# Merge products behind the sixth head, the first norm's weights spread by TensorE, and another order of the first transfers, in a two-layer encoder kernel

## The chip, the cores and the metric

The kernel runs on one core of one Trainium2 chip. The metric is the device time in microseconds of one execution, start to end. Several executions are timed and the median is taken; lower is better. One more execution is taken with the hardware profiler, and all rows in this document that are not of a timing come from such an execution.

## The reference

A trunk of two layers on 256 tokens of width 1024, all in float32. Cut to what matters:

```python
def reference(x, positions, norm_w, w_in, ...):
    angles = positions[..., None] * inv_freq
    cos, sin = jnp.cos(angles), jnp.sin(angles)
    for l in range(DEPTH):                                # DEPTH = 2
        h = rmsnorm(x, norm_w[l])                         # x: (1, 256, 1024)
        proj = h @ w_in[l]                                # one input projection for both branches
        (q_a, k_a, v_a, ab_a, z_a, q_b, k_b, v_b, z_b, gate_a, gate_b) = split(proj)
        y_a = gated_delta_branch(q_a, k_a, v_a, ab_a, z_a, ...)   # 8 heads, both directions, triangular solves
        y_b = diff_attention_branch(q_b, k_b, v_b, z_b, cos, sin, ...)  # 8 heads, two softmaxes each
        merged = sigmoid(gate_a) * (y_a @ w_pa[l]) + sigmoid(gate_b) * (y_b @ w_pb[l])
        x = x + merged @ w_out[l]
    return rmsnorm(x, final_norm_w)
```

`rmsnorm(x, w)` is `x * rsqrt(mean(x*x) + 1e-6) * w`.

## The kernel before, in words

Tokens are two tiles of 128 partitions (m = 0, 1). A projection multiplies the normalised, transposed input hT by 512 columns of weights. For precision each operand is split into a high and a low part in float32r, and three products are summed: high by high, high by low, low by high. Weights come in four parts of 512 KB (`raw`, three buffers). ScalarE (ACT) casts a part to its high half (line 233), VectorE (DVE) subtracts to get the low half (line 235), and TensorE (PE) runs 6 products of a token tile on a part, each 512 columns wide. A projection is 48 such products.

A planner orders the instructions of each engine from a simulated timeline. Program order is the priority, and within it a block `with behind(ins)` (or `tc.issue_after(ins)`) puts an instruction behind `ins` in the queue of the same engine. On the chip each engine runs its queue in that fixed order and waits by semaphores.

**The start.** SP's DMA queue issues, in this order: the two halves of token tile 0 (line 314), the norm's weights spread over all 128 partitions (`wb_n`, 512 KB, line 166), the two halves of tile 1, three weight parts of the first projection `vb` (line 224), and, once a buffer is free, the fourth part. `normed` squares a tile on ACT (line 177), adds the two sums on DVE (line 179), takes the power -0.5 on GpSimd (POOL, lines 161 and 162), and multiplies tile, factor and weights on DVE (line 189). `split_T` transposes on PE (line 199), copies the high part on ACT (205) and subtracts for the low part on DVE (206). `proj_by_tile` (line 261) then runs tile 0 over all eight row blocks (kt) and tile 1 after it, in that order on PE (line 275). The position arithmetic for the rotary embedding (lines 124 to 148) is small DVE work traced before all this.

**The merge.** In the middle of each layer, unit triangular blocks of 32 are solved on DVE (lines 619 and 620), written to device memory and read back in another layout, as `T64` (line 654) and `U_` (line 658). A generator `merges(g)`, one for each half of the heads, then joins blocks on PE: y64p (line 672), zt64 (686) and z64 (692), y128p (709), zt128 (717), each followed by copies on ACT. `step(mg)` advances both generators by one stage. Between the stages the attention heads stand, `head(h)`: scores `sc` (788), exponentials on ACT (797), transposes `at` (808), copy `aT` (810), the product with the values `av` (814). `mark["av"]` holds the last `av` product traced so far, `mark["proj"]` the last product of a projection. After the merge come `chunks`, the gated output, its transposes `pt_ya`, and the projection `pp_pa`; the projections `za`, `gb`, `pb` and `ga` supply PE's other work meanwhile.

## Time and profile before

| what | value |
|---|---|
| median of 3 runs | 793.67 us (792.81 to 794.49) |
| the profiled execution's own time | 795.0 us |
| its span, first to last instruction | 793.3 us |
| PE busy | 757.1 us, 95% of the span |
| DVE / ACT / POOL busy | 559.7 / 478.9 / 98.0 us |
| mean granted PE clock | 0.994 |
| DMA moved | 127.44 MB, 161 GB/s |

How to read rows: a timeline row is start, duration (us), engine, line, operation, output<-inputs, shape, count, and in brackets the idle time before it with what ended it. A wait row is "engine line waited for: total us, times, longest us". A chain row is start, length (us), engine and group. A tile's row of DMA issues gives the issuing queue's ns (min/median/max) and the first and last start in us, followed by a row of the time from issue to landing. A windows row is a stretch, its length, busy us of PE, PE's weight load, DVE, ACT and POOL with counts, granted clock, DMA share and GB/s.

### The profile page before, as it was taken

The page shows a single profiled execution, that of the slowest core. Times are in us where ns is not written, and L with a number is a line of the kernel's source. Part 1 is how long each engine was busy: PE and PEld are TensorE (multiplying, and loading weights), DVE is VectorE, ACT ScalarE, POOL GpSimd, SP SyncE. Part 2 cuts the span into 40 slices and gives each one's busy share as a digit, 9 for nine tenths or more (in the row PEclk, how much of TensorE's full clock was granted, in tenths as well). Part 3 has the DMA queues.
Part 4 walks back from the last instruction along what each step waited for, and adds up shares of the span by engine and source line. Part 5 has one row for each costly group of instructions (what it writes and reads, how often), then busy time and mean ns, then how long its engine had stood idle before and what let it go on. Part 6 is the DMA issues. An engine that isn't in the chain of part 4 may idle for free.

```text
span 793.3 us, 13809 instructions
## 1 busy us (share of the span) xinstructions
PE 757.1 (95%) x5218; PEld 650.0 (82%) x5218; DVE 559.7 (71%) x1053; ACT 478.9 (60%) x1043; POOL 98.0 (12%) x133
## 2 busy tenths in 40 slices
PE   4989999999999999999989899999999999999996
PEld 3988889887778988878769799799777789897874
DVE  5487978999973553666655978889999537447564
ACT  4557776556777655553534687765667775565443
POOL 6000371100030100100010015501001100001000
PEclk9999999999999999999999999999999999999999
DMA  6565757554494534355754467556455934435561
GB/s 200 166 186 147 199 178 209 160 171 146 111 206 126 159 127 133 107 178 183 224 166 129 143 181 242 159 171 174 146 159 140 196 99 154 132 110 158 184 208 58
DMA packets 77888, 127.44 MB, mean 161 GB/s; under 512 B 19694, under 2 KB 20030, under 8 KB 77822
## 3 DMA queue, kind: packets, MB, share of 16 engines
q1 hardware_dynamic: 73886, 116.79, 49.5%
q0 software_dynamic: 3936, 9.77, 4.6%
q8 instruction: 41, 0.67, 0.4%
q14 instruction: 25, 0.20, 0.1%
HBM read 121.79 MB, written 4.75 MB: 160 GB/s over the span
## 4 chain that ended last, share of the span: by engine, by line
PE 66%; DVE 14%; DMA 8%; ACT 7%; issue 3%; POOL 1%; SPq 0%; POOLq 0%; ACTq 0%; DVEq 0%
PE pp_qk L248 3%; PE pp_qk L249 3%; PE pp_vb L275 2%; PE pp_qk L247 2%; PE pf_v L290 2%; PE pp_gb L247 2%; ACT B L577 2%; PE pf_v L294 2%; PE pf_v L292 2%; PE pp_gb L248 2%; PE pp_pb L248 2%; PE pp_gb L249 2%; PE pp_pb L247 2%; PE pp_pb L249 2%; PE pf_k L294 2%
## 5 line engine op out<-in xcount | busy, mean ns | idle before, releaser
L248 PE MATMUL pp_qk<-lo_qk,hT 128*128 128x512 f32 x128 | 51.3, 401 | 1.0 <-DVE lo_qk L235 1.0
L249 PE MATMUL pp_qk<-hi_qk,hT 128*128 128x512 f32 x128 | 50.0, 391 | 0.0
L235 DVE TENSOR_TENSOR lo_qk<-raw_qk,hi_qk 128x1024 fp32r<-128x1024 f32 x32 | 40.2, 1256 | 9.0 <-ACT hi_qk L233 8.7
L247 PE MATMUL pp_qk<-hi_qk,hT 128*128 128x512 f32 x128 | 46.1, 398 | 0.4 <-ACT hi_qk L233 0.4
L233 ACT CAST hi_qk<-raw_qk 128x1024 fp32r<-128x1024 f32 x32 | 33.5, 1047 | 20.0 <-PE pp_qk L249 12.6
L235 DVE TENSOR_TENSOR lo_pb<-raw_pb,hi_pb 128x1024 fp32r<-128x1024 f32 x16 | 19.6, 1225 | 31.3 <-ACT hi_pb L233 31.3
L235 DVE TENSOR_TENSOR lo_gb<-raw_gb,hi_gb 128x1024 fp32r<-128x1024 f32 x16 | 19.6, 1223 | 30.2 <-ACT hi_gb L233 30.2
L290 PE MATMUL pf_v<-hT,hi_v 128*128 128x256 f32 x128 | 36.5, 288 | 0.0
L290 PE MATMUL pf_q<-hT,hi_q 128*128 128x256 f32 x128 | 36.3, 287 | 0.0
L292 PE MATMUL pf_v<-hT,hi_v 128*128 128x256 f32 x128 | 36.2, 285 | 0.0
L797 ACT ACTIVATE es<-sc,mx 128x256 f32<-128x256 f32 x64 | 29.8, 472 | 10.4 <-DVE mx L795 10.3
L292 PE MATMUL pf_q<-hT,hi_q 128*128 128x256 f32 x128 | 35.8, 284 | 0.0
L290 PE MATMUL pf_k<-hT,hi_k 128*128 128x256 f32 x128 | 35.6, 283 | 0.0
L292 PE MATMUL pf_k<-hT,hi_k 128*128 128x256 f32 x128 | 35.6, 283 | 0.0
L294 PE MATMUL pf_q<-hT,lo_q 128*128 128x256 f32 x128 | 35.2, 290 | 0.0
L294 PE MATMUL pf_v<-hT,lo_v 128*128 128x256 f32 x128 | 34.5, 285 | 0.0
L294 PE MATMUL pf_k<-hT,lo_k 128*128 128x256 f32 x128 | 34.3, 286 | 0.0
L235 DVE TENSOR_TENSOR lo_pa<-raw_pa,hi_pa 128x1024 fp32r<-128x1024 f32 x16 | 19.6, 1224 | 18.7 <-ACT hi_pa L233 18.7
L235 DVE TENSOR_TENSOR lo_k<-raw_k,hi_k 128x1024 fp32r<-128x1024 f32 x16 | 19.6, 1224 | 18.0 <-ACT hi_k L233 18.0
L235 DVE TENSOR_TENSOR lo_ga<-raw_ga,hi_ga 128x1024 fp32r<-128x1024 f32 x16 | 19.4, 1224 | 16.0 <-ACT hi_ga L233 16.0
L476 DVE SCALAR_TENSOR_TENSOR cvk<-pf_k,cw,cvk 128x254 f32<-128x254 f32 (+1 forms) x64 | 29.2, 478 | 2.0 <-ACT cvk L472 1.2
L233 ACT CAST hi_pa<-raw_pa 128x1024 fp32r<-128x1024 f32 x16 | 16.9, 1054 | 22.4 <-PE pp_pa L249 18.9
(361 smaller groups left out, 2520.9 us busy)
## 6 DMA issues: line engine op xcount, KB each, us to landing
raw_qk<-in_w_in_dram SPq DMA_DIRECT2D x32, 512.0 KB, 3.7
raw_vb<-in_w_in_dram SPq DMA_DIRECT2D x16, 512.0 KB, 3.8
raw_k<-in_w_in_dram SPq DMA_DIRECT2D x16, 512.0 KB, 3.7
raw_q<-in_w_in_dram SPq DMA_DIRECT2D x16, 512.0 KB, 3.7
raw_v<-in_w_in_dram SPq DMA_DIRECT2D x16, 512.0 KB, 3.8
raw_zb<-in_w_in_dram SPq DMA_DIRECT2D x16, 512.0 KB, 3.6
raw_za<-in_w_in_dram SPq DMA_DIRECT2D x16, 512.0 KB, 3.6
raw_gb<-in_w_in_dram SPq DMA_DIRECT2D x16, 512.0 KB, 4.2
```

What stands on the lines that cost most here:

```text
L233: S.copy(hi[:, :, :n], raw[:, :, :n])
L235: V.tensor_tensor(lo[:, :, :n], raw[:, :, :n], hi[:, :, :n].bitcast(F32), ALU.subtract)
L247: T.matmul(o, act[kt // 4][:, 0, kt % 4, ts_], hi, start=kt == 0, stop=False)
L248: T.matmul(o, act[kt // 4][:, 0, kt % 4, ts_], lo, start=False, stop=False)
L249: mark["proj"] = T.matmul(o, act[kt // 4][:, 1, kt % 4, ts_], hi, start=False, stop=kt == KT - 1).ins
L275: mark["proj"] = T.matmul(o, a_, w_, start=kt == 0 and a_ is ah and w_ is hi, stop=kt == KT - 1 and a_ is al).ins
L290: T.matmul(o, hi[:, cs], act[kt // 4][:, 0, kt % 4, :], start=first, stop=False, skip_group_check=True)
L292: T.matmul(o, hi[:, cs], act[kt // 4][:, 1, kt % 4, :], start=False, stop=False, skip_group_check=True)
L294: T.matmul(o, lo[:, cs], act[kt // 4][:, 0, kt % 4, :], start=False, stop=done, skip_group_check=True)
L476: V.scalar_tensor_tensor(ca[:, o0:o1], acc[:, b, o0 + sft : o1 + sft], cw[:, j, cb : cb + 1], ca[:, o0:o1], ALU.mult, ALU.add)
L577: S.activation(dec[:, d, j4, :], dec[:, d, j4, :], AF.Exp, bias=lnc[:, d, c, h : h + 1])
L797: S.activation(es[:, n, qt, :], spv[:, qt, :], AF.Exp, bias=mx[:, n, qt : qt + 1], accum_out=s_all[:, h, n, qt : qt + 1])
```

## The change

Three edits.

1. The first layer's norm weights are read as one row of 4 KB on ACT's DMA queue (`norm_row`), and two PE products with a row of ones spread it over the partitions into two PSUM banks. DVE reads them there. All other norms keep the spread transfer.
2. The first transfers and the order of the first projection. SP issues tile 0, weight part 0, tile 1 (`tokens(1)`, called when row block 2 is reached), weight part 1. Parts 2 and 3 are issued on ACT's queue behind tile 0's squares (`held`). Parts 1 and 3 take buffers of the tag `w4a` (`spare`), so that all four have a buffer at once. The order on DVE is written out: low half of part 0 behind tile 0's last norm product; low half of part 1 behind tile 0's last transposed low half; tile 1's sum and norm products behind the low half of part 1; low halves of parts 2 and 3 behind tile 1's last norm product. The position arithmetic and the memset of `U_` are traced after the first projection, the former behind tile 1's last norm product.
3. In the merge, `head(4)` and `head(5)` both stand before the third step, and the first y64p product of half 0 is put behind `mark["av"]` (head 5's last) instead of `mark["proj"]`.

```diff
+    def norm_row(w_row, nm):
+        row = work.tile([P, DM], F32, tag="w4c", name=f"wr_{nm}", bufs=3)
+        nc.scalar.dma_start(out=row[0:1, :], in_=w_row.unsqueeze(0))
+        wb = [bank(f"wb_{nm}{i}") for i in range(2)]
+        for i in range(2):
+            T.matmul(wb[i], tri[0:1, 0, :], row[0:1, 512 * i : 512 * i + 512], start=True, stop=True)
+        return wb
...
-        V.tensor_tensor(r, ss[:, 0:1], ss[:, 1:2], ALU.add)
+        with behind(after):
+            V.tensor_tensor(r, ss[:, 0:1], ss[:, 1:2], ALU.add)
...
+        sq = norm_factor(xt_, m, h, r, ss, range(2), after and mark["norm", 0][1])
...
+            with behind(after):
+                hh = V.scalar_tensor_tensor(h[:, cs], xt_[i][:, m, :], r, wb[i],
+                                            ALU.mult, ALU.mult).ins
...
+                if kp in spare:
+                    raw = work.tile([P, 2, 512], F32, tag="w4a", name=f"raw_{nm}{kp}", bufs=2)
+                else:
+                    raw = wpool.tile([P, 2, 512], F32, tag="raw", name=f"raw_{nm}{kp}", bufs=3)
+                with behind(mark["norm", 0][0] if kp in held else None):
+                    (nc.scalar if kp in held else nc.sync).dma_start(
+                        out=raw[:, :, :n], ...)
...
+        if l == 0:
+            later[0] = None, mark["norm", 0][1]
+            def between(kt):
+                if kt == 2:
+                    tokens(1)
+                    later[1] = None, mark["split", 0, 1][1]
+                elif kt == 4:
+                    prenorm(1, xt, wb, 0, mark["parts"])
+                    later[2] = later[3] = None, mark["norm", 1][1]
...
         for _ in proj_by_tile(hT, wl, C_VB, evac_v(0), f"vb{l}0", places,
-                              later=later, turn=...):
+                              later=later, spare=() if l else (1, 3), held=() if l else (2, 3), between=between,
+                              turn=...):
...
-            first = mark["proj"] if g == 0 else None
+            first = mark["av"] if g == 0 else None
...
         step(mg)
         step(mg)
-        step(mg)
         head(4)
+        head(5)
         step(mg)
         step(mg)
         step(mg)
-        head(5)
+        step(mg)
         in_step(chunks(0), chunks(1))
```

More of the change, by code (lines that the diff above doesn't have):

```diff
@@ L123, in hybrid_encoder @@
         G.dma_start(out=pos_i, in_=positions.rearrange("o (m p) -> p (o m)", p=P))
-    pos_f = const.tile([P, NM], F32, name="pos_f")
-    V.tensor_copy(pos_f, pos_i)
-    freq = const.tile([P, RD], F32, name="freq")
-    for i, f in enumerate(INV_FREQ):
-        V.memset(freq[:, i : i + 1], f)
-    ang = const.tile([P, NM, RD], F32, name="ang")
-    for m in range(NM):
-        V.tensor_scalar(ang[:, m, :], freq, pos_f[:, m : m + 1], None, ALU.mult)
-    turns = const.tile([P, NM, RD], F32, name="turns")
-    turns_i = const.tile([P, NM, RD], I32, name="turns_i")
-    V.tensor_scalar(turns, ang, 1.0 / (2.0 * math.pi), None, ALU.mult)
-    V.tensor_copy(turns_i, turns)
-    V.tensor_copy(turns, turns_i)
-    for c in (TWO_PI_A, TWO_PI_B, TWO_PI_C):
-        V.scalar_tensor_tensor(ang, turns, -c, ang, ALU.mult, ALU.add)
-    PI_IN = 3.1415925
-    V.tensor_scalar(ang, ang, PI_IN, -PI_IN, ALU.min, ALU.max)
-    sin = const.tile([P, NM, RD], F32, name="sin")
-    cos = const.tile([P, NM, RD], F32, name="cos")
-    ang2 = const.tile([P, NM, RD], F32, name="ang2")
-    over = const.tile([P, NM, RD], F32, name="over")
-    V.tensor_scalar(ang2, ang, math.pi / 2, None, ALU.add)
-    V.tensor_scalar(over, ang2, math.pi, None, ALU.is_gt)
-    V.scalar_tensor_tensor(ang2, over, -2.0 * math.pi, ang2, ALU.mult, ALU.add)
-    V.tensor_scalar(ang2, ang2, PI_IN, -PI_IN, ALU.min, ALU.max)
     def e4(name, tag):
@@ L166, in norm_weights @@
         nc.sync.dma_start(out=wb, in_=w_row.partition_broadcast(P))
-        return wb
+        return [wb[:, :512], wb[:, 512:]]
     def norm_tiles(nm, m):
@@ L172, in norm_tiles, with norm_factor @@
                 small.tile([P, 2], F32, tag="xss", name=f"xss_{nm}{m}"))
-    def norm_factor(xt_, m, h, r, ss, halves_):
+    def norm_factor(xt_, m, h, r, ss, halves_, after=None):
         for i in halves_:
@@ L178, in norm_factor, with normed @@
                               accum_out=ss[:, i : i + 1]).ins
-        V.tensor_tensor(r, ss[:, 0:1], ss[:, 1:2], ALU.add)
+        with behind(after):
+            V.tensor_tensor(r, ss[:, 0:1], ss[:, 1:2], ALU.add)
         rsqrt_rows(r, r, 1.0 / DM, 1)
         return sq
-    def normed(xt_, wb, m, nm):
+    def normed(xt_, wb, m, nm, after=None):
         h, r, ss = norm_tiles(nm, m)
-        sq = norm_factor(xt_, m, h, r, ss, range(2))
+        sq = norm_factor(xt_, m, h, r, ss, range(2), after and mark["norm", 0][1])
         for i in range(2):
             cs = slice(512 * i, 512 * i + 512)
-            hh = V.scalar_tensor_tensor(h[:, cs], xt_[i][:, m, :], r, wb[:, cs],
-                                        ALU.mult, ALU.mult).ins
+            with behind(after):
+                hh = V.scalar_tensor_tensor(h[:, cs], xt_[i][:, m, :], r, wb[i],
+                                            ALU.mult, ALU.mult).ins
         mark["norm", m] = sq, hh
@@ L215, in behind, with weights @@
         return nullcontext() if ins is None else tc.issue_after(ins)
-    def weights(w, c0, n, nm, homes=(None,) * 4, ahead=True, later=None):
+    def weights(w, c0, n, nm, homes=(None,) * 4, ahead=True, later=None, spare=(), held=()):
         for kp in range(4):
@@ L222, in weights @@
             with tc.high_priority(offset=HP) if ahead and homes[kp] is None else nullcontext():
-                raw = wpool.tile([P, 2, 512], F32, tag="raw", name=f"raw_{nm}{kp}", bufs=3)
-                nc.sync.dma_start(
-                    out=raw[:, :, :n],
-                    in_=w[kp * 256 : (kp + 1) * 256, c0 : c0 + n].rearrange("(k p) c -> p k c", p=P))
                 if homes[kp] is not None:
@@ L231, in weights @@
                     lo = wpool.tile([P, 2, 512], F32R, tag="lo", name=f"lo_{nm}{kp}", bufs=2)
+                if kp in spare:
[4 more added lines that the diff above has]
+                    (nc.scalar if kp in held else nc.sync).dma_start(
+                        out=raw[:, :, :n],
+                        in_=w[kp * 256 : (kp + 1) * 256, c0 : c0 + n].rearrange("(k p) c -> p k c", p=P))
                 with behind(act):
@@ L234, in weights @@
                 with behind(dve):
-                    V.tensor_tensor(lo[:, :, :n], raw[:, :, :n], hi[:, :, :n].bitcast(F32),
-                                    ALU.subtract)
+                    mark["parts"] = V.tensor_tensor(lo[:, :, :n], raw[:, :, :n],
+                                                    hi[:, :, :n].bitcast(F32), ALU.subtract).ins
             for k in range(2):
@@ L259, in homes, with proj_by_tile @@
                 yield t_[:, k]
-    def proj_by_tile(act, w, c0, evac, nm, places, later=None, turn=None):
+    def proj_by_tile(act, w, c0, evac, nm, places, later=None, turn=None, spare=(), held=(), between=None):
         accs = banks2(f"pp_{nm}")
-        ws = list(weights(w, c0, 512, nm, places, ahead=False, later=later))
+        ws = []
+        parts = weights(w, c0, 512, nm, places, ahead=False, later=later, spare=spare, held=held)
+        if between is None:
+            ws.extend(parts)
         for m in range(NM):
@@ L268, in proj_by_tile @@
             o = accs[m]
-            for kt, hi, lo in ws:
+            for kt in range(KT):
+                if len(ws) == kt:
+                    if between and kt % 2 == 0:
+                        between(kt)
+                    ws.append(next(parts))
+                hi, lo = ws[kt][1:]
                 if kt == 6 and turn and turn(m):
@@ L308, in srcdst, with tokens, prenorm @@
         return (2 * mm, 2 * mm + 1) if d == 0 else (2 * mm + 1, 2 * mm)
+    U_ = big.tile([P, 2, 16, P], F32, name="U_")
+    wb = norm_row(norm_w[0], "n0")
     xt = e4("xt0", "ex")
     xdr = x[0].rearrange("(m p) (i d) -> p i m d", p=P, i=2)
-    for m in range(NM):
+    def tokens(m):
         for i in range(2):
             nc.sync.dma_start(out=xt[i][:, m, :], in_=xdr[:, i, m, :])
-        if m == 0:
-            wb = norm_weights(norm_w[0], "n0")
-    def prenorm(m, xt_, wb_, l_):
-        h = normed(xt_, wb_, m, f"n{l_}")
+    tokens(0)
+    def prenorm(m, xt_, wb_, l_, after=None):
+        h = normed(xt_, wb_, m, f"n{l_}", after)
         for i in range(2):
@@ L324, in hybrid_encoder @@
     hT = pair("hT0")
-    for m in range(NM):
-        prenorm(m, xt, wb, 0)
-    U_ = big.tile([P, 2, 16, P], F32, name="U_")
-    norms = mark["pow"]
-    with tc.issue_after(norms):
-        G.memset(U_, 0.0)
+    prenorm(0, xt, wb, 0)
     for l in range(DEPTH):
@@ L347, in hybrid_encoder @@
         places = list(homes((("A", 1), ("ktm", 1), ("vtm", 1), ("B", 1)), f"vb{l}"))
-        later = None
-        if l:
+        later, between = {}, None
+        if l == 0:
[7 more added lines that the diff above has]
+                    later[2] = later[3] = None, mark["norm", 1][1]
+        else:
             later = {2: mark["norm", 0], 3: mark["split", 0, 0]}
@@ L352, in hybrid_encoder @@
         for _ in proj_by_tile(hT, wl, C_VB, evac_v(0), f"vb{l}0", places,
-                              later=later, turn=lambda m: None if m or not l else mark["turn", 1, 0]):
-            pass
+                              later=later, spare=() if l else (1, 3), held=() if l else (2, 3), between=between,
+                              turn=lambda m: None if m or not l else mark["turn", 1, 0]):
+            pass
+        if l == 0:
+            norms = mark["pow"]
+            with tc.issue_after(norms):
+                G.memset(U_, 0.0)
+            pos_f = const.tile([P, NM], F32, name="pos_f")
+            with tc.issue_after(mark["norm", 1][1]):
+                V.tensor_copy(pos_f, pos_i)
+            freq = const.tile([P, RD], F32, name="freq")
+            for i, f in enumerate(INV_FREQ):
+                V.memset(freq[:, i : i + 1], f)
+            ang = const.tile([P, NM, RD], F32, name="ang")
+            for m in range(NM):
+                V.tensor_scalar(ang[:, m, :], freq, pos_f[:, m : m + 1], None, ALU.mult)
+            turns = const.tile([P, NM, RD], F32, name="turns")
+            turns_i = const.tile([P, NM, RD], I32, name="turns_i")
+            V.tensor_scalar(turns, ang, 1.0 / (2.0 * math.pi), None, ALU.mult)
+            V.tensor_copy(turns_i, turns)
+            V.tensor_copy(turns, turns_i)
+            for c in (TWO_PI_A, TWO_PI_B, TWO_PI_C):
+                V.scalar_tensor_tensor(ang, turns, -c, ang, ALU.mult, ALU.add)
+            PI_IN = 3.1415925
+            V.tensor_scalar(ang, ang, PI_IN, -PI_IN, ALU.min, ALU.max)
+            sin = const.tile([P, NM, RD], F32, name="sin")
+            cos = const.tile([P, NM, RD], F32, name="cos")
+            ang2 = const.tile([P, NM, RD], F32, name="ang2")
+            over = const.tile([P, NM, RD], F32, name="over")
+            V.tensor_scalar(ang2, ang, math.pi / 2, None, ALU.add)
+            V.tensor_scalar(over, ang2, math.pi, None, ALU.is_gt)
+            V.scalar_tensor_tensor(ang2, over, -2.0 * math.pi, ang2, ALU.mult, ALU.add)
+            V.tensor_scalar(ang2, ang2, PI_IN, -PI_IN, ALU.min, ALU.max)
         cw_rows = work.tile([TAPS * 24, P], F32, tag="cwr", name=f"cwr{l}", bufs=1)
@@ L966, in hybrid_encoder @@
             S.activation(h[:, 512:], xt[0][:, m, :], AF.Square, accum_out=ss[:, 0:1])
-            V.tensor_tensor(h[:, :512], xt[0][:, m, :], wb[:, :512], ALU.mult)
+            V.tensor_tensor(h[:, :512], xt[0][:, m, :], wb[0], ALU.mult)
         if more:
@@ L979, in hybrid_encoder @@
                 S.activation(hv[:, 0], hv[:, 0], AF.Copy, scale=r)
-                V.scalar_tensor_tensor(hv[:, 1], xt[1][:, m, :], r, wb[:, 512:], ALU.mult, ALU.mult)
+                V.scalar_tensor_tensor(hv[:, 1], xt[1][:, m, :], r, wb[1], ALU.mult, ALU.mult)
                 for i in range(2):
```

## The prediction

> **What bounds the kernel now.** I read the page first (busy shares, the chain that ended last), then TensorE's own waits, and then the timeline at the places that these waits name.

> ```profile
> span 793.3 us, 13809 instructions
> PE 757.1 (95%) x5218; PEld 650.0 (82%) x5218; DVE 559.7 (71%) x1053; ACT 478.9 (60%) x1043; POOL 98.0 (12%) x133
> PE 66%; DVE 14%; DMA 8%; ACT 7%; issue 3%; POOL 1%; SPq 0%; POOLq 0%; ACTq 0%; DVEq 0%
> PE pt_h L199 <- DVE h_n L189: 11.7, 3, 9.0
> PE y64p L672 <- DMA T<-udr: 3.2, 2, 1.9
> ```

> TensorE is busy 757.1 of 793.3 us and carries two thirds of the chain, so time is won only where it idles or runs slowly. The two longest entries among its waits are the places that the change touches: 11.7 us before the transposes of the normalised input, 9.0 of it at the very start, and 3.2 us in two waits, one a layer, before the merge's first products y64p.

> **The start as it is.** The timeline of the first 45 us:

> ```profile
> 0.80 0.86 SPq L314 DMA_DIRECT2D xt<-in_x_dram  x2
> 4.91 0.16 DVE L179 TENSOR_TENSOR xr_n<-xss_n 128x1 f32<-128x1 f32 x1 [1.81 <-ACT h_n L177]
> 5.43 0.57 POOL L162 TENSOR_TENSOR xr_n<-rspre,mhalf 128x1 f32<-128x1 f32 x1
> 8.23 1.41 DVE L189 SCALAR_TENSOR_TENSOR h_n<-xt,xr_n,wb_n 128x512 f32<-128x512 f32 x2 [0.85 <-DMA wb_n<-in_norm_w_dram]
> 9.04 1.97 PE L199 MATMUL pt_h<-ident,h_n 128*128 128x128 f32 x8 [9.04 <-DVE h_n L189]
> 11.08 0.68 DVE L206 TENSOR_TENSOR hT<-pt_h,hT 128x512 fp32r<-128x512 f32 x1
> 12.51 1.05 ACT L233 CAST wktm_vb<-raw_vb 128x1024 fp32r<-128x1024 f32 x1
> 19.22 1.23 DVE L235 TENSOR_TENSOR wB_vb<-raw_vb,wB_vb 128x1024 fp32r<-128x1024 f32 x1 [1.13 <-ACT wB_vb L233]
> ```

> The factor of the first tile is ready at 6.0 (5.43 + 0.57), but its product with the weights starts only at 8.23, when the spread row wb_n has landed. The transfers, by tile (issue, and time to landing in us):

> ```profile
> L166 SPq DMA_DIRECT2D wb_n<-in_norm_w_dram x1: 424/424/424, 1.7 to 1.7; - x1
> DMA to landing us min/median/max: 6.4/6.4/6.4
> L314 SPq DMA_DIRECT2D xt<-in_x_dram x4: 388/426/432, 0.8 to 2.7; - x4
> DMA to landing us min/median/max: 2.7/4.9/7.1
> L224 SPq DMA_DIRECT2D raw_vb<-in_w_in_dram x4: 387/452/1867, 3.1 to 14.4; - x4
> DMA to landing us min/median/max: 3.7/8.4/9.7
> L224 SPq DMA_DIRECT2D raw_vb<-in_w_in_dram x2: 469/1168/1867, 3.6 to 4.1; - x2
> DMA to landing us min/median/max: 8.8/9.3/9.7
> pos_i<-in_positions_dram POOLq DMA_DIRECT2D x1, 1.0 KB, 5.7
> ```

> The second half of the first tile is issued at 1.24 and lands near 4.1, wb_n at 1.7 + 6.4 = 8.1, the second tile's last half at 2.7 + 7.1 = 9.8, the second and third weight parts at 3.6 + 8.8 = 12.4 and 4.1 + 9.7 = 13.8. So late half-megabytes follow each other by 1.4 us, while the spread row holds the queue 4.0 us. The fourth part, issued at 14.4 once a buffer was free, lands at 14.4 + 3.7 = 18.1; its low half is done on VectorE at 20.45 (19.22 + 1.23). The chain from there:

> ```profile
> 14.45 2.93 PE pp_vb L275 x6
> 17.37 0.85 PE pt_h L199 x4
> 19.94 7.99 PE pp_vb L275 x35
> 262.51 1.78 PE y1p L733 x16
> 274.25 0.87 PE pt_yb L199 x8
> ```

> The first projection ends at 27.93 (19.94 + 7.99); one product costs 7.99 / 35 = 0.228 us. The last two rows are prices: eight float32 products 128 wide take 1.78 us (0.22 each, two records per product), eight transposes 0.87. At the start four transposes take 0.85 and eight 1.97: TensorE is at half speed there, until about 18, though the clock row reads full.

> **The change, first part: the start.** *Removed*: the spread transfer and its 4.0 us of SP's queue. *Added*: one 4 KB row on ACT's queue, ahead of the table load there, and two one-row products, 512 wide. At 4 x 0.22 they are 0.89 each at full speed and 1.78 at the half speed seen here. The row is issued near 0.8; its landing lies between 2.7 us after (xt) and 5.7 (pos_i), 3.5 to 6.5; I take 3.7, nearest to xt, whose queue is of the same hardware kind. The halves of wb are then in PSUM at 5.5 and 7.3. TensorE is idle then, so the products cost nothing but this delay. *Moved on SP's queue*: the first weight part now stands ahead of the second tile. With wb_n gone: part one 4.1 + 1.4 = 5.5, second tile 6.9, part two 8.3. *Moved to ACT's queue*: parts three and four, each with a buffer of its own, issued behind the first tile's squares, near 4.9 and 5.3. That delays ACT by two issues of 0.4 (1.9 at worst, the longest issue above), covered because ACT's next work, the cast of part one, waits for 5.5. They share the engines with part two: alone it lands at 8.3, and if both queues share evenly from 5.5 on, four half-megabytes later, at 11.1. ACT's data should flow about 2 us after issue (xt: 2.7 us, of which 0.7 is half of 1.4), so from 6.9: I take 9.7.

> [...]

> VectorE's order is now fixed, and it sets the end. By the rows above (0.75 per half product, 1.22 per low half, 0.68 per transposed low half, 1.1 from sum to factor): products of tile 1 at 6.0 to 6.75 and, waiting for wb's second half, 7.3 to 8.05; low half of part one to 9.3; two transposed low halves to 10.7; low half of part two (cast on ACT by 9.7 + 1.05) to 12.0; only now the sum and factor of the second tile, which the change queues behind it, to 13.1; its products to 14.6; low half of part three to 15.8; transposed low halves of tile 2 to 17.2; low half of part four to 18.4. The position arithmetic (a score of ops of about 0.17) now stands behind; I allow 0.3 for what slips in: 18.7. TensorE then has 29 products, 29 x 0.228 = 6.6: end at 25.3. It idles some 2.4 us before part three, and a 1.89 us stall halved its clock elsewhere (next part), so 0.3 for a half-speed remnant: 25.6 instead of 27.93. **Start: -2.3 us.** Bounds: row at 6.5 costs 2.8 more (+0.5); part two at 11.1 costs 1.4 (-0.9); part four's low half ahead of the transposed ones, no allowance: -4.3. The gain carries on, because TensorE waits for nothing long until the stall below, and later parts have free buffers earlier. The small POOL transfers stand behind the second tile's factor as before (11.6, now 13.1), so 1.5 later; I count that as hidden behind the products up to 25.6, and it costs up to 1.5 if ACT or VectorE then stands waiting for one of them.

> **Second part: the merge.** *Moved*: head 5 ahead of the first products, whose first is now held behind that head's last product (av) instead of the projection's. No instruction and no DMA is added.

> ```profile
> 234.12 0.71 PE L247 MATMUL pp_za<-hi_za,hT 128*128 128x512 f32 x2
> 234.40 0.59 ACT L810 COPY aT<-at 128x512 f32<-128x512 f32 x1 [0.61 <-PE at L808]
> 236.72 1.79 PE L672 MATMUL y64p<-T,A 32*32 32x32 f32 x128 [1.89 <-DMA T<-udr]
> 238.52 2.00 PE av L814 x8
> 243.01 0.72 PE L686 MATMUL zt<-U__187,y 32*32 32x32 f32 x62
> 625.13 1.33 PE L672 MATMUL y64p<-T,A 32*32 32x32 f32 x128 [1.36 <-DMA T<-udr]
> 626.47 1.09 PE av L814 x8
> 237.50:238.50 1.00, 1.00 (x78) 0.94 (x67) 0.00 (x0) 0.80 (x3) 0.00 (x0) 0.50 1.24 142
> L658 SPq DMA_DIRECT2D U__187<-udr x1: 886/886/886, 236.0 to 236.0; - x1
> DMA to landing us min/median/max: 4.7/4.7/4.7
> ```

> Counting scores and transposes before it, the av right behind y64p is head 5's; its input aT is ready at 235.0. TensorE stands from 234.83 to 236.72 although this work is ready. With av first it runs 235.0 to 236.1 and y64p still starts at 236.7; behind the new wait stand only the remaining products of the za projection, which stood behind y64p's wait before. There is a second gain in layer 0: the granted clock is 0.50 (the windows row, whose last three columns are clock, DMA share and GB/s) just after the 1.89 us stall, and y64p with av takes 1.79 + 2.00 there against 1.33 + 1.09 in layer 1, whose 1.36 us stall lies in stretches at 1.00. With 0.8 us left I expect no drop. Layer 0: both are through at 236.72 + 1.33 = 238.05 instead of 240.52, -2.47. Layer 1: 626.46 instead of 627.56, -1.1. [...]

> What is late next: zt, which reads U_. Its first product would come at 243.01 - 2.47 = 240.5; the last U_ transfer lands at 236.0 + 4.7 = 240.7. I take back 0.2, and 0.1 in layer 1, where the same sum comes out nearly level. **Merge: -3.3 us.** Bounds: 0 (y64p's wait turns up at zt) and -4.6 (both stalls whole, 3.2, and the 1.4 of slow clock).

> **Sum.** -2.3 - 3.3 = -5.6. The profiled execution took 795.0 us around its span of 793.3; it becomes 789.4 with a span of 787.7. The runs' median is 793.67, 1.33 under the profiled one: 793.67 - 5.6 = **788.1**.

> **Rivals.**
> *The row is late*: it lands like pos_i, the start gains nothing (+0.5), the merge's 3.3 stay: 790.9. For: a small transfer took 5.7. Against: that was another queue. Chance 0.13.
> *The shared queues*: part two at 11.1 or a little later (12.4, where it landed before, makes the start -2.3 + 2.7 = +0.4): with the merge 789.5 to 790.8. For: more bytes are in flight at once. Against: SP's queue alone was not full after 4. Chance 0.15.
> *The change doesn't do what it says at the merge*: the planner puts av in front and the wait shows up at zt, or the stall was a matter of the clock's phase: 793.67 - 2.3 = 791.4. Chance 0.12.
> *Slower*: y64p, now of lower rank than head 5, is placed behind head 6 too. The next av comes here:

> ```profile
> 249.68 1.16 PE L814 MATMUL av<-vb,aT 128*128 128x128 f32 x8
> 343.02 1.03 PE L199 MATMUL pt_ya<-ident,kq 128*128 128x128 f32 x8
> 352.07 0.61 PE L247 MATMUL pp_pa<-hi_pa,yaT 128*128 128x512 f32 x2
> ```

> That is 249.68 - 238.5 = 11.2 later. The merge's chain is serial up to pt_ya, and the work that covers its end is what TensorE does between the last pt_ya (to 344.05) and pp_pa at 352.07, 8.0, less some 1.3 for the last copy and subtraction: 6.7. Beyond it each us costs one: 11.2 - 6.7 = 4.5 a layer, 9.0 in all, against the start's -2.3: 800.4. It decides against the change from 6.7 + 1.15 = 7.9 us of delay. Against: y64p needs only head 5. Chance 0.05.

> **How the numbers follow.** My forecast has the remaining 0.55; its own range is 785.5 to 790. The whole range reaches to the merge rival, with 791.8 at its top; the low end is both bounds nearly together (-4.3 and -4.6 would be 784.8): 785.2. Within 0.2%, about what this kernel's measurement can tell from no change (792.1 to 795.3), the first four cases lie only when two of them meet: a late row and a void merge together give 793.67 + 0.5 = 794.2. I put 0.10 on such pairs, out of the 0.95 of these cases, which leaves 0.85 for faster; slower is the 0.05 of its rival.

> **What would show it.** First transposes near 6.8 to 7.4 instead of 9.04; pp_vb's last product near 25.6; the low half of part two right after its cast (else the shared queues), the first h_n after 6.0 waiting for wb (else not); av of head 5 in front of y64p, a stall of 0.8 and 0.3 there, the clock at 1.00, no new wait at zt. I am wrong if a wait of an engine in these stretches is long and named otherwise, or if TensorE gets idle time later that pays the gain back.

## The result: 0.6% slower, and the profile after

The changed kernel takes 798.53 us (median of 20 executions, 792.97 to 803.44), the kernel before beside it 793.29 (20 executions): ratio 1.0058, 95% interval 1.0040 to 1.0075. The forecast was 788.1. The profiled execution of the changed kernel took 794.83 us, one of its shortest; the last paragraph of this section says why it hides the loss.

Of the changed kernel, the engines' busy times and the queue of instruction transfers (number, MB, share), both from the page, and then some of TensorE's waits (engine, line, waited for: total us, times, longest us):

```profile
PE 761.3 (96%) x5222; PEld 650.4 (82%) x5222; DVE 559.1 (70%) x1053; ACT 479.9 (61%) x1043; POOL 99.3 (13%) x133
...
q8 instruction: 41, 0.67, 0.4%
```

```profile
PE zt L726 <- issue: 3.5, 2, 3.1
PE wb_n L145 <- POOL tri L113: 3.1, 1, 3.1
...
PE pt_h L185 <- DVE h_n L175: 2.0, 3, 1.4
...
PE sc L828 <- issue: 1.6, 1, 1.6
PE pp_vb L276 <- ACT hT L191: 1.2, 1, 1.2
PE pp_vb L276 <- DVE wktm_vb L227: 1.2, 1, 1.2
```

The two entries that I had read in the kernel before (11.7 us at the start, 3.2 us for T) are gone or small, as intended, although at the start 3.1 us now stand before the spread products and 2.4 us before the first projection's. New are 5.1 us (3.5 + 1.6) whose releaser is "issue": TensorE waited for nothing that the profile names. I call these unnamed stalls; they lie in the merges. TensorE's timeline there, and the same stretches as windows (length, busy us of PE, PEld, DVE, ACT, POOL, then granted clock, DMA share, GB/s):

```profile
237.80 1.05 PE L854 MATMUL av<-vb,aT 128*128 128x128 f32 x8
238.78 1.33 PE L712 MATMUL y64p<-T,A 32*32 32x32 f32 x128
240.48 0.71 PE L726 MATMUL zt<-U__96,y 32*32 32x32 f32 x62 [0.38 <-issue]
...
242.73 1.13 PE L828 MATMUL sc<-qkT 64*128 64x256 f32 x7
245.49 0.48 PE L828 MATMUL sc<-qkT 64*128 64x256 f32 x1 [1.63 <-issue]
...
623.59 1.05 PE L854 MATMUL av<-vb,aT 128*128 128x128 f32 x8
624.57 1.33 PE L712 MATMUL y64p<-T,A 32*32 32x32 f32 x128
626.23 0.54 PE L726 MATMUL zt<-U__96,y 32*32 32x32 f32 x38 [0.33 <-ACT y L716]
629.85 0.47 PE L726 MATMUL zt<-U__96,y 32*32 32x32 f32 x17 [3.09 <-issue]
```

```profile
245.50:249.40 3.90, 3.90 (x106) 3.61 (x106) 2.66 (x8) 2.82 (x11) 0.58 (x1) 0.56 0.51 138
...
624.50:626.60 2.10, 1.77 (x168) 1.59 (x166) 0.00 (x0) 1.71 (x7) 0.00 (x0) 1.00 1.05 391
626.60:629.90 3.30, 0.21 (x21) 0.10 (x13) 0.00 (x0) 0.00 (x0) 0.00 (x0) 0.76 0.32 115
629.90:636.20 6.30, 6.30 (x159) 4.71 (x161) 2.23 (x3) 4.16 (x9) 0.00 (x0) 0.59 0.01 3
```

Three things are to be seen. y64p waits for T no more, but it starts at 238.78, 2.1 us later than before: the planner did not put only av ahead of it. zt now follows it directly, where av and eleven products of za stood between; in the kernel before, the last of these eleven is

```profile
242.69 0.39 PE L247 MATMUL pp_za<-hi_za,hT 128*128 128x512 f32 x1
```

And TensorE stops in the middle of zt for 3.09 us while VectorE, ScalarE and GpSimd stand as well (busy times 0.00 from 626.60 to 629.90), and then has a mean granted clock of 0.59 for 6.3 us.

**What "issue" is here.** The DMA table has queues of their own for instructions; one of them, q8, has 41 transfers of 16 KB. TensorE has 10,540 instructions in the trace (10,444 weight loads and products and 96 semaphore and drain instructions, in order of start), one transfer of q8 for 257 of them. I numbered them from 0 in every trace. All twelve unnamed stalls over 0.5 us in the merges, in ten traces, stand at a number that is 193 above a multiple of 256: 3009, 3265, 8385 or 8641. So I read that TensorE has run to the end of a block of 256 and the next block is not there. In the changed kernel the block behind 3264 is requested at 242.97 and TensorE goes on at 245.49; the one behind 8384 is requested at 627.61 and TensorE goes on at 629.85. In the trace, between 627.5 and 629.9, TensorE's transfer is one of very few packets:

```profile
q1 hardware_dynamic: 27, 0.04, 6.0%
q8 instruction: 1, 0.02, 2.6%
```

Over all twelve stalls it takes 2.2 to 3.2 us from the request to TensorE's next instruction. At the 0.228 us that a product and its load take in the first projection before (7.99 us for 35), a block lasts 29 us by estimate; y64p is 256 instructions and takes 1.3 us. The table has all kernels: the median and ratio of the timings (each against the kernel before beside it; e1 to e4 ran on one chip, e5 to e12 on another), and from one profiled execution each, in us, the start of abq (a small product that comes soon after the first projection), the time from the last zb product to the first pp_pa (the stage that holds the merge), the unnamed stalls over 0.5 us, and the stretches with a granted clock of 0.50 between 100 us and the last 10.

| kernel | median | ratio (95%) | abq starts | last zb to pp_pa, layer 0 | same, layer 1 | unnamed stalls: us at number | half clock inside |
|---|---|---|---|---|---|---|---|
| before | 793.29 | | 33.0 | 144.8 | 142.8 | none | 3.4 + 3.4 |
| after | 798.53 | 1.0058 (1.0040, 1.0075) | 31.3 | 144.6 | 146.8 | 1.63 at 3265, 3.09 at 8385 | 3.4 + 6.8 |
| e1 start only | 795.08 | 1.0041 (1.0021, 1.0061) | 32.1 | 146.1 | 143.0 | 2.08 at 3009 | 3.4 + 3.4 |
| e2 merge only | 795.80 | 1.0037 (1.0024, 1.0049) | 33.3 | 143.1 | 146.3 | 0.70 at 3265, 2.96 at 8385 | 3.4 |
| e3 after again | 798.10 | 1.0061 (1.0042, 1.0080) | 33.3 | 143.1 | 146.9 | 3.08 at 8385 | 6.8 |
| e4 gb loads late | 800.44 | 1.0099 (1.0077, 1.0121) | 33.2 | 146.9 | 146.2 | 1.22 at 8385 | 3.4 + 6.8 |
| e5 start, padded | 792.73 | 0.9997 (0.9981, 1.0013) | 32.8 | 142.8 | 142.1 | none | 3.4 |
| e6 merge spaced | 791.63 | 0.9974 (0.9955, 0.9993) | 34.3 | 141.7 | 141.7 | none | 3.4 |
| e7 e6 padded | 792.05 | 0.9991 (0.9975, 1.0008) | 33.8 | 142.0 | 143.1 | 0.91 at 8385 | none |
| e8 e7, parts on SP | 789.22 | 0.9949 (0.9933, 0.9965) | 32.1 | 142.4 | 143.4 | 1.28 at 8641 | none |
| e9 e6, parts on SP | 789.60 | 0.9952 (0.9935, 0.9970) | 31.0 | 142.9 | 141.7 | 1.07 at 3009 | none |
| e10 e9, squares late | 793.98 | 1.0013 (0.9996, 1.0029) | 34.1 | 146.5 | 141.7 | none | 3.4 |
| e11 merge spaced only | 793.44 | 1.0004 (0.9985, 1.0023) | 32.9 | 145.3 | 141.7 | 0.67 at 3009 | 3.4 |
| e12 two products more | 794.03 | 1.0011 (0.9992, 1.0029) | 32.4 | 144.2 | 141.8 | 1.80 at 3009 | none |

The four kernels with zt right behind y64p (after, e2, e3, e4) need 146.2 to 146.9 for layer 1's stage, the ten others 141.7 to 143.4: about 4 us, nearly the whole loss. The profiled pair doesn't show it in its spans: the changed kernel gains 1.8 at the start and 0.2 in layer 0's stage, loses 4.0 in layer 1's, and gains 3.1 between the two (241.1 instead of 244.2), where the execution of before had a stretch of half clock at 400.9 us and this one none. In the twelve other traces that part takes 241.5 to 245.3, under either order.

### The profile page after: what moved, and what is told of

Read it like the earlier page. It is cut to its first block, busy times and chain, and to the rows that moved or that the text cites. A ratio compares the mean times of both kernels' runs of the same rounds, so it can differ in the third digit from the quotient of the medians.

```text
span 793.1 us, 13823 instructions
## 1 busy us (share of the span) xinstructions
PE 761.3 (96%) x5222; PEld 650.4 (82%) x5222; DVE 559.1 (70%) x1053; ACT 479.9 (61%) x1043; POOL 99.3 (13%) x133
## 3 DMA queue, kind: packets, MB, share of 16 engines
q10 hardware_dynamic: 546, 1.05, 0.4%
## 4 chain that ended last, share of the span: by engine, by line
PE 74%; DVE 10%; DMA 6%; ACT 5%; issue 3%; SPq 0%; POOL 0%; POOLq 0%; ACTq 0%; DVEq 0%
DMA raw_q<-in_w_in_dram 3%; PE pp_qk L240 2%; PE pp_qk L241 2%; PE sc L828 2%; PE pp_qk L239 2%; PE pp_vb L276 2%; PE av L854 2%; PE pf_v L291 2%; PE pp_za L240 2%; PE pf_v L295 2%; PE pp_za L241 2%; PE pf_v L293 2%; PE pp_gb L240 2%; PE pp_gb L241 2%; PE pp_gb L239 2%
## 5 line engine op out<-in xcount | busy, mean ns | idle before, releaser
L227 DVE TENSOR_TENSOR lo_pa<-raw_pa,hi_pa 128x1024 fp32r<-128x1024 f32 x16 | 19.6, 1224 | 18.7 <-ACT hi_pa L225 18.7
```

The costliest lines, as they stand in the source:

```text
L227: mark["parts"] = V.tensor_tensor(lo[:, :, :n], raw[:, :, :n], hi[:, :, :n].bitcast(F32), ALU.subtract).ins
```

## The experiments

Theory A: the start gains a little, and the merge edit loses because two runs of tiny instructions (y64p and zt) now stand back to back and outrun the fetch of TensorE's own instructions. Its rival B: the start edit costs. A rival within A: the fetch is late because it shares the DMA engines with weights (A1), or it would be late anyway (A2).

**e1, start only.** The changed kernel, merge as before:

```diff
-            first = mark["av"] if g == 0 else None
+            first = mark["proj"] if g == 0 else None
...
-        head(4)
-        head(5)
         step(mg)
+        head(4)
...
         step(mg)
+        head(5)
```

> The changed kernel with the merge as it was: head 5 behind the sixth step again, the first products held behind the projection. Theory A (the start gains, the merge loses): the first norm's transposes, the first projection and the landmark product abq come as early as in the changed kernel (abq starts near 31.3 instead of 33.0), y64p waits for T again (about 1.9 and 1.4 us), and the time is 1 to 2.5 us below the kernel before, about 791.5, ratio 0.997 to 0.999. Rival B (the start is what costs, through its other order of transfers and of VectorE's work): ratio 1.004 to 1.008, as the changed kernel.

Measured: 1.0041, slower. So far rival B has it. But its trace has the start 0.9 us earlier, not later, and loses in layer 0's merge:

```profile
234.83 1.33 PE L712 MATMUL y64p<-T,A 32*32 32x32 f32 x128 [1.04 <-DMA T<-udr]
236.09 1.16 PE L854 MATMUL av<-vb,aT 128*128 128x128 f32 x8
237.00 0.48 PE L240 MATMUL pp_za<-lo_za,hT 128*128 128x512 f32 x1
239.56 0.59 PE L241 MATMUL pp_za<-hi_za,hT 128*128 128x512 f32 x1 [2.08 <-issue]
239.94 0.63 PE L240 MATMUL pp_za<-lo_za,hT 128*128 128x512 f32 x1
```

An unnamed stall of 2.08 us at number 3009, and half clock behind it (0.63 for a product that takes 0.40 in e12 below). The order of this stretch is the one of before. What differs is that the two products which spread the row are eight instructions (the page counts 5222 weight loads and 5222 products, against 5218 of each before), so everything behind them has moved by eight towards the end of its block. My theory had said nothing of that.

**e2, merge only**, the same three places edited the other way in the kernel before.

> The kernel before with the merge edit alone. Theory A: y64p's wait for T is gone, but TensorE stands at zt or sc in both layers with nothing that the profile names to wait for (1.6 us in layer 0 and about 3 in layer 1 in the changed kernel's profile), the granted clock falls to half behind it, and the time is 5 to 8 us above the kernel before: 798 to 801, ratio 1.006 to 1.010. Rival B: ratio 0.995 to 0.999, since the merge edit then gains its stall.

Measured: 1.0037, slower, by less than the expected 1.006 to 1.010, and the clock fell to half in layer 1 alone. Both parts lose by themselves.

```profile
PE zt L686 <- issue: 4.0, 3, 3.0
```

**e3, the changed kernel again.**

> The changed kernel itself, unaltered, beside the others on the same chip. Theory A: ratio 1.004 to 1.0075 as measured; run to run it spreads wider than the kernel before (by 5 us or more), because what it loses hangs on the moment at which TensorE's next instructions come in. Rival (one bad profile, no real loss): ratio within 0.998 to 1.002.

Measured: 1.0061, the same loss. Its abq is at 33.3 instead of 31.3, with not an instruction changed. The wider spread that was expected did not show: 3.5 us over its six executions, 4.6 over the 23 of the kernel before.

**e4, raw_gb late.**

```diff
-                with behind(mark["norm", 0][0] if kp in held else None):
-                    (nc.scalar if kp in held else nc.sync).dma_start(
+                late = nm.startswith("gb") and nm.endswith("0") and kp < 3
+                with behind(mark["y64c"] if late else mark["norm", 0][0] if kp in held else None):
+                    (nc.scalar if kp in held or late else nc.sync).dma_start(
...
-            S.copy(y64, y64p)
+            mark["y64c"] = S.copy(y64, y64p).ins
```

> The changed kernel with the first three weight transfers of raw_gb (three half-megabytes a layer) issued on ACT's queue behind the last copy of y64 instead of on SP's queue, where they are under way while y64p runs. In the changed kernel's profile the transfer of TensorE's own instructions that holds what comes behind zt begins in layer 1 only when these loads are through, 2.7 us after TensorE has passed into its last block. Theory A1 (the transfer of instructions waits behind the weights): the unnamed stall of 3.1 us in layer 1 shrinks below 1 us, the one of layer 0 (1.6 us) stays or shrinks, and the time is 791 to 795. Theory A2 (y64p and zt run through a block faster than any transfer comes, whatever else is under way): stalls of 1 to 3 us stay in both layers and the time stays near 798. Rival C (zt waits for the landing of U_): the stall stays, and lies right behind the landing.

Measured: 1.0099. The stall of layer 1 shrank, to 1.22 where A1 had said below 1, and the one of layer 0 is gone. The time rose instead of falling, since the late weights are now waited for (pp_gb, and ScalarE's work ahead of av):

```profile
PE av L855 <- ACT aT L851: 1.9, 1, 1.9
...
PE zt L727 <- issue: 1.6, 2, 1.2
PE pp_gb L240 <- ACT es L838: 1.6, 2, 1.3
```

In layer 1 of the changed kernel TensorE passes number 8128 at 624.90 and the fetch starts at 627.61, 2.7 us later, when the three loads (391 GB/s above) have nearly run out. In e4 it passes at 630.58 and the fetch starts at 631.47, 0.9 later; the stall falls from 3.09 to 1.22. So by this pair of executions 1.8 us of it went with the three loads, and 1.2 remain: both A1 and A2, in parts.

**e5, start only, padded.** e1 and, ahead of the spread products,

```diff
+    def pads(n):
+        for _ in range(n):
+            T.matmul(padp, padt, padt, start=True, stop=True)
...
+    padt = const.tile([32, 32], F32, name="padt")
+    V.memset(padt, 0.0)
+    padp = bank_c("padp")[0:32, 0:32]
+    pads(12)
```

> The start edit alone, as in e1_start_only, and ahead of the first norm's products twelve small float32 products (32 by 32, into a bank that nobody reads), in TensorE's idle start: they add 48 instructions to its stream and nothing to the result. In all five traces so far each unnamed stall of TensorE stands at the instruction whose number (weight loads and products counted together) is 193 above a multiple of 256, where a new block of its instructions begins; in e1_start_only that was 3009, just behind y64p and av, and cost 2.1 us and a stretch at half clock. Theory A (where the blocks begin decides): y64p now begins 30 instructions behind a block's beginning instead of 18 ahead of it, so the next block is there in time; no unnamed stall over 0.5 us, and the ratio falls from 1.004 to 0.996 to 1.000 (789 to 792.5). Rival B (the start edit costs by its transfers and VectorE's order): ratio stays 1.003 to 1.006.

Measured: 0.9997 against e1's 1.0041. Twelve products that compute nothing are worth about 3.5 us (0.0044 of 793; the intervals do not meet, though the two ran on different chips, each beside the kernel before). All behind them lies 48 instructions further on in its block, and the unnamed stall is gone. This refutes B for the loss, and also shows that the start edit as built gains nothing that can be measured.

**e6, the merge spaced out.** In the changed kernel:

```diff
+                mark["proj", kt, m] = mark["proj"]
...
-            first = mark["av"] if g == 0 else None
+            first = mark["proj", 5, 0] if g == 0 else None
...
-            first = mark["av"]
+            first = mark["proj", 7, 0]
...
-        step(mg)
-        step(mg)
-        step(mg)
-        step(mg)
+        z_part(za, C_ZA, "za", 1)
+        with tc.high_priority(offset=HP):
+            step(mg)
+            step(mg)
+            step(mg)
+            step(mg)
         in_step(chunks(0), chunks(1))
-        z_part(za, C_ZA, "za", 1)
```

The first mark puts y64p behind the 33rd of za's 48 products, the second puts zt behind the 45th.

> The changed kernel with the merge spaced out as the prediction had meant it: the first products y64p held behind the 33rd of the 48 products of the second half of za (they stood behind the 46th in the changed kernel and behind the 26th in the kernel before), and zt behind the 45th. So nine products of za stand ahead of y64p instead of two, and av and twelve products of za between y64p and zt. No wait for T over 0.4 us. Theory A: y64p begins 4 instructions ahead of instruction 2752 in layer 0, where a block ends, and the next block ends 4 instructions behind y64p, so an unnamed stall of 1.5 to 2.5 us stands there, at number 3009 (in av); none in layer 1; ratio 0.998 to 1.004. If instead merely the back-to-back y64p and zt cost, whatever the blocks: no stall in either layer, ratio 0.993 to 0.997.

Measured: 0.9974, and no unnamed stall over 0.5 us in either layer; the stage is 141.7 in both, as short as any. y64p waits for nothing:

```profile
237.80 1.33 PE L713 MATMUL y64p<-T,A 32*32 32x32 f32 x128
```

The expected stall at 3009 did not come, although y64p begins 4 instructions ahead of 2752, and the time is near what was expected if only y64p and zt back to back cost. That y64p alone can run into a block's end is shown by e1 above and e9, e11 and e12 below. In e6 the fetch started at 236.70, 1.1 us before TensorE reached number 2752, and came in time. In e1 it started at 236.36, 1.5 us after that number was passed. My explanation is the wait for T, 1.04 us just ahead of y64p in e1 and none in e6. How such a wait would hold up a fetch is not shown. The traces group that way: with a wait for T just ahead of number 2752 the fetch starts 1.1 to 1.5 us behind it (before, e1, e12), without one from 1.2 us ahead to 0.2 behind (e10, e6, e11, e9).

**e7, e6 with eight products of padding.**

> e6_spaced with eight small products (32 instructions) in TensorE's idle start, so that y64p begins 28 instructions behind the block's beginning in layer 0. Theory A: no unnamed stall over 0.5 us in either layer, no half clock in the merges, ratio 0.993 to 0.997 (787 to 790). Rival (the fetch is late for another reason than the place of the block): the stall of e6_spaced stays.

Measured: 0.9991, above the expected 0.993 to 0.997. Layer 0 is as expected; layer 1 has 0.91 at 8385, which I had not expected. e6 and e7 can't be told apart by their intervals.

**e8, e7 with parts three and four on SP's queue.**

```diff
-                              later=later, spare=() if l else (1, 3), held=() if l else (2, 3), between=between,
+                              later=later, spare=() if l else (1, 3), held=(), between=between,
```

> e7_spaced_pad with the third and fourth weight parts of the first projection on SP's queue behind the second part again (each still with a buffer of its own). In four traces of the changed start the first part's cast begins at 7.6, 7.7, 9.4 and 9.5, where 5.5 was predicted, and the second tile's squares and the copy of the first transposes stand behind it on ACT; TensorE waits 1.2 to 3.3 us for that copy. Theory A (parts three and four on ACT's queue take bandwidth from part one): the cast of part one begins by 7.0, TensorE's wait for the copy is under 1.2 us, the landmark product abq begins at or before 31.3 (31.3 to 33.3 in the four traces), and the time is 0.5 to 2 us below e7_spaced_pad. Rival (part one is late because the tokens and the row stand ahead of it, or by the chance of the transfers' phase): the cast stays at 7.6 to 9.5, the time is that of e7_spaced_pad within 0.5 us.

Measured: 0.9949, 2.8 us below e7, with e9 the fastest of all. But the reason given is wrong: the first cast still begins at 9.50. What went is the wait for part two's low half (1.2 to 1.6 us in six of the seven other traces of this start). Part two lands 1.4 us behind the second tile here (1.3 in e9), and 2.4 to 2.9 us behind it in those six: with two queues it comes later, as the prediction's rival of the shared queues had it. (In the seventh, e1, it was 1.4 on two queues as well.)

**e9, e8 without the padding.**

> e8_spaced_pad_sp without the eight small products: the start of the change with parts three and four on SP's queue, and the merge spaced out. e6_spaced, whose instructions lie the same, had no unnamed stall in either layer, because nothing makes TensorE's instruction stream wait just ahead of y64p, so the fetch of the next block starts 1.1 us before its boundary; e8 had 0.4 and 1.3 us in layer 1. Theory A: no unnamed stall over 0.5 us in either layer, time 787 to 789.5, ratio 0.992 to 0.995. Rival (the small products helped by their place): stall back at number 3009 in layer 0, ratio 0.996 to 1.000.

Measured: 0.9952, at the upper end of the expected time, with a stall of 1.07 at 3009, against what was expected. This time the fetch started 0.2 us behind the boundary, not 1.1 ahead, and y64p started at 234.58, 3.2 us sooner than in e6; why the fetch did not start sooner as well is not shown. The stalls of this kernel are not at an end.

```profile
234.58 1.33 PE L713 MATMUL y64p<-T,A 32*32 32x32 f32 x128
235.84 0.49 PE L855 MATMUL av<-vb,aT 128*128 128x128 f32 x2
237.40 0.83 PE L855 MATMUL av<-vb,aT 128*128 128x128 f32 x6 [1.07 <-issue]
```

**e10, squares late.** e9 and, in `norm_factor`,

```diff
         for i in halves_:
-            sq = S.activation(h[:, 512 * i : 512 * i + 512], xt_[i][:, m, :], AF.Square,
-                              accum_out=ss[:, i : i + 1]).ins
+            with behind(mark["split", 0, 0][0] if after else None):
+                sq = S.activation(h[:, 512 * i : 512 * i + 512], xt_[i][:, m, :], AF.Square,
+                                  accum_out=ss[:, i : i + 1]).ins
```

> e9_spaced_sp with the second tile's two squares held on ACT behind the copy of the first tile's first transposes (ACT's order before: cast of part one, two squares, that copy). In eight traces of the changed start TensorE waits 1.2 to 3.4 us for that copy, and the two squares are 1.2 us of it. Theory: the first pp_vb starts 0.6 to 1.2 us sooner behind the cast of part one (2.8 us behind the start of that cast in the eight traces), the rest follows, 0.3 to 1.2 us below e9. Rival: the second tile's chain then ends the start, pt_h of tile two waits longer and the time is that of e9 within 0.3 us.

Measured: 1.0013, 4.4 us above e9. The step itself is as expected (the first pp_vb 1.6 us behind the start of part one's cast, 11.21 after 9.62, instead of 2.8), but the planner, given other times, put y128p, zt, and y1p of layer 0 closer behind each other (3 products of gb instead of 12 between the two runs of y128p, none instead of 5 between those of zt), and layer 0's stage is 146.5:

```profile
PE pp_ga L241 <- DVE lo_ga L228: 2.7, 2, 2.2
...
PE zt L759 <- ACT y L753: 1.2, 1, 1.2
```

As a test of the start it is inconclusive.

**e11, spaced merge on the kernel before**, with two products of padding.

> The kernel before with the spaced merge alone (y64p behind nine products of za, av and twelve products of za ahead of zt), and two small products in the idle start, which bring the instructions ahead of y64p to within one of e6_spaced. Theory A: the waits for T (1.9 and 1.4 us) are gone or under 0.4, no unnamed stall over 0.5; 1.5 to 3.5 us below the kernel before, ratio 0.9955 to 0.998. Rival (the wait moves to zt or later in the serial chain): 0.999 to 1.001.

Measured: 1.0004. Layer 1's stage is 141.7 as in e6, but layer 0 got the same other order as e10 (1.5 us at zt, 1.7 at pp_ga) and needs 145.3. So this run does not show a gain of spacing by itself: layer 1's 141.7 is no shorter than the 141.8 of e12, which has the old order, and e6's time contains the new start too.

**e12, two products more.** The kernel before with two of e5's products at the start, nothing else.

> The kernel before with nothing but two small float32 products (8 instructions, 32 by 32, into a bank that nobody reads) ahead of TensorE's idle start: as many instructions as the spread row's products add to the changed kernel. Theory A: y64p still waits for T, now 19 instructions ahead of the block's end instead of 27, av follows it up to number 3005 or so, and the block that begins at 3009 is not yet there: an unnamed stall of 0.5 to 2.5 us at 3009 in layer 0, ratio 1.0015 to 1.005. Rival (eight instructions that cost 0.1 us in idle time cannot matter): no such stall, ratio 0.999 to 1.001.

```profile
234.37 1.56 PE L680 MATMUL y64p<-T,A 32*32 32x32 f32 x128 [0.62 <-DMA T<-udr]
235.86 1.16 PE L822 MATMUL av<-vb,aT 128*128 128x128 f32 x8
236.78 0.48 PE L252 MATMUL pp_za<-lo_za,hT 128*128 128x512 f32 x1
239.05 0.40 PE L253 MATMUL pp_za<-hi_za,hT 128*128 128x512 f32 x1 [1.80 <-issue]
```

Measured: the stall stands at 3009 as foretold, 1.80 us, in a stretch whose order is that of before. The time, 1.0011, lies between the two expectations, and its interval holds 1: in this execution the clock did not drop, and the stall overlaps what T's wait and the slow clock had cost.

## Why the prediction was wrong, step by step

**The merge, forecast -3.3, measured +3.5 to +4.1 in layer 1 and -1.7 to -0.2 in layer 0 (after, e2, e3).** The step that failed is "With av first it runs 235.0 to 236.1 and y64p still starts at 236.7". The planner, with head 5 traced earlier, placed av behind twenty more products of za (46 of the 48 stood ahead of y64p instead of 26). What had hidden the time from y64p to zt was used up ahead of y64p. I called that "only the remaining products" and did not ask what they covered. The second missing piece is a resource that I did not price: the supply of instructions. "No instruction and no DMA is added" holds for the products and weight loads of the merge (5,218 of each in before and in e2) and is beside the point, since the same instructions in another order outran it; and at the start I priced the time of the two spread products, not that their eight instructions shift all that follow. "No new wait at zt" was the sign that I had named, and there the wait stands.

Where the code does what I had supposed, T's wait goes: in e6 nine products of za cover it (I had thought of av), and av and twelve more products stand ahead of zt. The stages are there 144.8 - 141.7 = 3.1 and 142.8 - 141.7 = 1.1 us shorter than in the profiled execution of before, near the prediction's -2.47 and -1.1. But these prices were those of one execution. In the four traces with the old order T's waits in the two layers are 1.9 and 1.4 us (before), 1.0 and 0.8 (e1), 0.9 and 0.6 (e5), 0.6 and 0.2 (e12), and half clock follows such a wait in the first alone. Against e5, which has the old order and no unnamed stall (142.8 and 142.1), e6 is shorter by 1.1 and 0.4 only. So the merge term was also too large: 3.3 stood for a wait that differs from execution to execution.

**The clock.** "With 0.8 us left I expect no drop" was about a stall that no longer exists; the new ones of 1.63 and 3.09 go with 3.4 and 6.8 us at half clock. My estimate from the traces is that this costs TensorE another 1.7 and 2.6 us, half of what remains of each stretch when it works again (3.4 and 5.3 us). The drops between 100 us and the last 10 last one or two times 3.4 us in every trace that has any, but they come after stalls of 1.2 us (e4) and stay away after 1.80 (e12), so the length of a stall alone did not decide. What did, a phase of the clock, as one rival had it, or something else, no run shows.

**The start, forecast -2.3, measured -1.8 in the profiled execution and nothing on average.** The seven traces with this start have abq at 31.3 to 34.3, mean 33.0; the four with the old one 32.4 to 33.3, mean 32.9. The first projection itself, forecast to end at 25.6 instead of 27.93, ends at 27.41 in the changed kernel's trace and at 29.1 on average of the seven, against 27.8 of the four. The row was as early as forecast and better: the spread products run from 3.10 to 6.88, and the transposes start at 7.25 instead of 9.04, within the forecast 6.8 to 7.4, although the factor of the first tile is ready at 6.4 instead of 6.0. The failed step is "the spread row holds the queue 4.0 us", and from it "part one 4.1 + 1.4 = 5.5". Windows of before and after over the same microseconds:

```profile
4.00:6.00 2.00, 0.00 (x0) 0.00 (x0) 0.16 (x1) 0.88 (x4) 0.75 (x2) 1.00 0.52 167
...
8.00:10.00 2.00, 0.96 (x5) 0.96 (x6) 1.73 (x5) 0.95 (x3) 0.00 (x0) 1.00 1.04 399
```

```profile
4.00:6.00 2.00, 2.00 (x4) 0.66 (x2) 0.16 (x1) 1.09 (x4) 0.34 (x2) 1.00 0.91 155
```

From 4 to 6 us the DMA moves 143 to 252 GB/s in all fourteen kernels, whatever is queued, against 399 from 8 to 10 here. Those microseconds are slow, not that transfer, and no run shows why; with the spread row gone, part one spends them in its stead. The second step that failed is that ACT is "covered": the copy of the first transposes stands on ACT behind the cast of part one and both squares of tile two, so TensorE waits for that landing too.

```profile
7.63 1.04 ACT L225 CAST wA_vb<-raw_vb 128x1024 fp32r<-128x1024 f32 x1 [2.35 <-DMA raw_vb<-in_w_in_dram]
8.59 0.62 ACT L161 ACTIVATE h_n<-xt 128x512 f32<-128x512 f32 x1
...
9.83 0.56 ACT L191 CAST hT<-pt_h 128x512 fp32r<-128x512 f32 x1
11.54 1.04 ACT L225 CAST wktm_vb<-raw_vb 128x1024 fp32r<-128x1024 f32 x1 [1.15 <-DMA raw_vb<-in_w_in_dram]
```

That cast begins at 7.5 to 9.6 in the ten traces of the changed start, not at 5.5; part two's at 11.54 here, past even the bound of 11.1, where I had 9.7. With parts three and four on SP's queue (e8, e9) the wait for part two's low half was gone, and e8 is 2.8 us below e7, e9 2.0 below e6 (the latter two intervals overlap).

**The rivals.** The sign came from a way that none of them named. The slower rival had y64p late by a head, 800.4; y64p was late by 2.1 us only, and the stage lost by what followed it. What stays open: what makes the request at number 8128 in layer 1 come 0.9 us behind the boundary in e4 and 3.8 in e7. In e7 the DMA is full (352 GB/s from 623.2 to 625.2 us) until about the time of the request at 625.22, as it is in the changed kernel, but only e4 moved the loads away; whether they are the cause in e7 no run shows.

## What to carry to other kernels

A wait named "issue" in the middle of a run of tiny products is worth a count: number TensorE's instructions, and if the stalls share a remainder of 256, as all twelve did here (193), the fetch of instructions is a likely bound there. Here long products between the tiny ones helped (no unnamed stall in e6), and a shift of the whole stream by 48 instructions took one stall out (e5); neither is a sure cure, since a shift by 32 left a stall in layer 1 (e7) and the spaced merge one in layer 0 (e9). A wait that is to be removed should be read from more than one execution: T's wait was 1.9 us in one and 0.6 in another of the same order. When a transfer is seen to be slow, look at whether its neighbours in time are slow as well before its removal is given a price. And a hint to a planner is not an order: what it places next to the edit has to be read from the new list, since the work that filled the old wait was covering another.

The spaced merge with all weight parts on SP's queue (e9, 789.60 us; with padding e8, 789.22) is faster than the kernel before by 0.5% (0.9952, 0.9935 to 0.9970), where the changed kernel is slower by 0.6%.
